# A softmax with relative-position bias: one row of one chunk loaded in 16 transfers of 15 to 1 partitions, first chunk in one transfer, bias table loaded once per 8 partitions

## The chip, the cores and the metric

One core of a Trainium2 chip runs the kernel. Its engines are VectorE (DVE in the profile), ScalarE (ACT), GpSimd (POOL), SyncE (SP) and TensorE (PE, not used here), and 16 DMA engines move data between HBM and the on-chip memory of 128 partitions. The metric is the device time in microseconds (us) of one execution; times of several runs are given as their median.

## What is computed

```python
B, H, S = (2, 8, 2112); max_rel = 16
rel = pos[:, None] - pos[None, :]
rel_clipped = np.clip(rel, -max_rel, max_rel) + max_rel
bias = rel_bias[:, rel_clipped]            # rel_bias: H x 33
logits = logits + bias[None]               # logits: B x H x S x S, float32
logits = logits - logits.max(axis=-1, keepdims=True)
exp = np.exp(logits)
return exp / exp.sum(axis=-1, keepdims=True)
```

It is a softmax over rows of 2112 elements, with a bias that depends on the head and on the distance between row and column, clipped at 16. Every element of the logits is read once and every element of the result is written once.

## The kernel before

The B x H x S = 33,792 rows are shared out evenly: each of the 128 partitions has ROWS = 264 consecutive rows of one head (PB = 8 partitions for each head and batch). A row is S = 2112 float32, 8448 bytes. The work goes in N = 44 chunks of R = 6 rows per partition; a chunk of all partitions is 6336 KB. Four buffers X[0] to X[3] (NBUF = 4) take the chunks in turn, and all is done in place.

**Order of the transfers.** All loads and stores are issued by SP, in program order. Before its loop SP issues the loads of the first four chunks. In the loop it issues the store of chunk n + 1 as soon as its rows are scaled (`store` takes the semaphore `scaled`), waits until the store of chunk n has landed (`st[b]`), and issues the load of chunk n + 4 into that buffer (`load`). The last chunk is stored in two halves.

**The first chunk** is loaded with six transfers of one row per partition (line 88). Five of them count on the semaphore `pre`, the sixth on `ld[0]`. VectorE takes `pre` before its loop (line 190), so it begins its loop when five rows are there. The other chunks come with one transfer each (line 78) that counts on `ld[b]`. Every transfer raises its semaphore by 16 in all when it has landed.

**The bias table.** ScalarE issues one transfer that copies the whole 8 x 33 table to each of the 128 partitions, into the tile F (line 97). GpSimd makes two small index tables. From these VectorE makes masks, keeps the head of each partition by a multiplication (line 131) and a sum over the heads (line 135, into rbS, 33 values), and builds the table M in the accumulation memory (lines 139 to 155): for each partition, the bias of every distance between row and column that occurs. `then` counts each instruction on the semaphore `dve` and `settle` waits for all so far.

**The loop.** VectorE, once for four chunks, copies a window of M to F (`strip`, line 160), so that each row's bias is a slice of F. Then for each chunk: `add` waits for `ld[b]` and runs one instruction per row that adds the bias and makes the row's negated maximum (line 166); ScalarE (`exps`, line 175) makes the exponential and its sum; `scale` on VectorE makes the reciprocals of three rows (line 183) and multiplies the rows by them (line 187).

Of the kernel before, what the change touches and what calls it, by code (L numbers as in the profile page):

```python
# [15 lines left out]
def kernel(  # L16
# [6 lines left out]
    nc = tc.nc  # L23
    P = 128
    B, H, S, S2 = logits.shape
    assert S == S2
    MR = 16
    W = 2 * MR + 1
    ROWS = B * H * S // P
    PB = S // ROWS  # L30
    assert ROWS * P == B * H * S and PB * ROWS == S and PB == H == 8
    R = 6
    NBUF = 4
# [4 lines left out]
    MW = S + ROWS - 1  # L38
    FW = S + STEP - 1
    BIG = 3.0e38  # L40

    io = ctx.enter_context(tc.tile_pool(name="io", bufs=1))
    X = [io.tile([P, R * S], FP32, tag=f"X{b}", name=f"X{b}") for b in range(NBUF)]
    F = io.tile([P, FW], FP32, tag="F", name="F")
    rbS = io.tile([P, W], FP32, tag="rbS", name="rbS")
# [3 lines left out]
    ip = io.tile([P, 3, PB], I32, tag="ip", name="ip")  # L49
# [3 lines left out]
    def view(t, offset, dims):  # L53

        return bass.AP(tensor=t.tensor, offset=t.offset + offset, ap=[[list(t.ap[0])[0], P]] + dims)

    def rows(t, j, n):

        return bass.AP(tensor=t.tensor, offset=t.offset + j * S, ap=[[ROWS * S, P], [1, n * S]])

    with tc.tile_critical(no_gpsimd_drain=True):
        ld = [nc.alloc_semaphore(f"ld{b}") for b in range(NBUF)]
# [3 lines left out]
        scaled = nc.alloc_semaphore("scaled")  # L66
        inv = nc.alloc_semaphore("inv")
        rb = nc.alloc_semaphore("rb")
        pre = nc.alloc_semaphore("pre")
        idx = nc.alloc_semaphore("idx")  # L70
        dve = nc.alloc_semaphore("dve")

        def take(eng, sem, n):
            eng.wait_ge(sem, n).then_inc(sem, -n)  # L74


        def load(j, b):
            nc.sync.dma_start(out=X[b][:, :], in_=rows(logits, j, R)).then_inc(ld[b], 16)
# [5 lines left out]
            ).then_inc(st[b], 16)  # L84


        for r in range(R):
            nc.sync.dma_start(
                out=X[0][:, r * S : (r + 1) * S], in_=rows(logits, r, 1)
            ).then_inc(ld[0] if r == R - 1 else pre, 16)  # L90
        for n in range(1, NBUF):
            load(n * R, n)

        rbB = view(F, 0, [[1, H * W]])
        nc.scalar.dma_start(
            out=rbB,
            in_=bass.AP(tensor=rel_bias.tensor, offset=rel_bias.offset, ap=[[0, P], [1, H * W]]),
        ).then_inc(rb, 16)  # L100
        nc.gpsimd.iota(ip[:, 0], pattern=[[0, PB]], base=0, channel_multiplier=1).then_inc(idx, 1)
        nc.gpsimd.iota(ip[:, 2], pattern=[[1, PB]], base=0, channel_multiplier=0).then_inc(idx, 1)  # L102

        v = nc.vector
        done = [0]

        def then(ins):
            done[0] += 1
            ins.then_inc(dve, 1)

        def settle():
            v.wait_ge(dve, done[0])

        SC = H * W
        mask = [F[:, SC + i * PB : SC + (i + 1) * PB] for i in range(9)]
        dp, dh, eq, hm, gt, le, lt, ra, rz = mask
        v.wait_ge(idx, 2)
        then(v.tensor_scalar(out=ip[:, 1], in0=ip[:, 0], scalar1=3, scalar2=7,  # L118
                             op0=ALU.logical_shift_right, op1=ALU.bitwise_and))
# [7 lines left out]
        for m, op in ((eq, ALU.is_equal), (gt, ALU.is_gt), (le, ALU.is_le), (lt, ALU.is_lt)):  # L127
# [4 lines left out]
            out=view(F, 0, [[W, H], [1, W]]), in0=view(F, 0, [[W, H], [1, W]]),  # L132
            in1=view(F, SC + 3 * PB, [[1, H], [0, W]]), op=ALU.mult))
        settle()
        then(v.tensor_reduce(out=rbS[:, :], in_=view(F, 0, [[1, W], [W, H]]),  # L135
                             axis=mybir.AxisListType.X, op=ALU.add))
        settle()
        low, high = rbS[:, W - 1 : W], rbS[:, 0:1]
        then(v.tensor_scalar(out=ra, in0=gt, scalar1=low, scalar2=None, op0=ALU.mult))  # L139
        then(v.tensor_scalar(out=rz, in0=gt, scalar1=low, scalar2=None, op0=ALU.mult))  # L140
        then(v.tensor_tensor(  # L141
            out=view(F, 0, [[W, PB], [1, W]]), in0=view(F, SC + 2 * PB, [[1, PB], [0, W]]),
            in1=view(rbS, W - 1, [[0, PB], [-1, W]]), op=ALU.mult))
# [6 lines left out]
            out=view(M, U, [[ROWS, PB], [1, W]]), in0=view(F, 0, [[W, PB], [1, W]]),  # L150
            in1=view(F, SC + 8 * PB, [[1, PB], [0, W]]), op=ALU.add))
        then(v.tensor_copy(out=view(M, U + W, [[ROWS, PB], [1, ROWS - W]]),  # L152
                           in_=view(F, SC + 7 * PB, [[1, PB], [0, ROWS - W]])))
        then(v.tensor_copy(out=M[:, 0:U], in_=low.to_broadcast([P, U])))  # L154
# [7 lines left out]
        def add(b):  # L162
            take(v, ld[b], 16)
            for r in range(b * R, (b + 1) * R):
                x = X[b][:, (r - b * R) * S : (r - b * R + 1) * S]
                v.tensor_tensor_reduce(  # L166
                    out=x, in0=x, in1=F[:, STEP - 1 - r : STEP - 1 - r + S], scale=-1.0, scalar=BIG,
                    op0=ALU.add, op1=ALU.min, accum_out=nmax[:, r : r + 1],
# [18 lines left out]
                    v.tensor_scalar_mul(out=x, in0=x, scalar1=rec[:, r : r + 1]).then_inc(scaled, 1)  # L187

        v.sem_inc(dve, -done[0])
        take(v, pre, 16 * (R - 1))  # L190
        with nc.Fori(0, ROWS - STEP + 1, STEP, engines=[ENG.DVE]) as j:  # L191
            strip(j)
            take(v, dve, 1)
# [51 lines left out]
```

## Time and profile before

| | |
|---|---|
| median of 3 runs | 1331.43 us (1330.2 to 1332.81) |
| span of the profiled execution, first to last instruction | 1327.7 us |
| VectorE busy | 976.6 us (74%) |
| ScalarE busy | 575.2 us (43%) |
| moved by the DMA engines | 571.11 MB, mean 430 GB/s over the span |
| HBM read, written | 285.61 MB, 285.47 MB |

The profile is of one execution. Its page gives the span of that execution and no device time of its own, so the span is the time that the lines add up to; the median of the runs is 3.7 us above it. In the page's slices each digit is the busy share of a fortieth of the span in tenths. The share of the DMA engines in a window is that of the packets that begin in it, so a short window can show over 1.00. A packet here is one contiguous piece that one DMA engine moves, or the 4 bytes with which it tells a semaphore that its part of a transfer is done.

### The profile page before, as it was taken

The page shows a single profiled execution, that of the slowest core. Times are in us where ns is not written, and L with a number is a line of the kernel's source. Part 1 is how long each engine was busy: PE and PEld are TensorE (multiplying, and loading weights), DVE is VectorE, ACT ScalarE, POOL GpSimd, SP SyncE. Part 2 cuts the span into 40 slices and gives each one's busy share as a digit, 9 for nine tenths or more (in the row PEclk, how much of TensorE's full clock was granted, in tenths as well). Part 3 has the DMA queues.
Part 4 walks back from the last instruction along what each step waited for, and adds up shares of the span by engine and source line. Part 5 has one row for each costly group of instructions (what it writes and reads, how often), then busy time and mean ns, then how long its engine had stood idle before and what let it go on. Part 6 is the DMA issues. An engine that isn't in the chain of part 4 may idle for free. (4 is left out here: it accounts for less than half of the span.)

```text
span 1327.7 us, 2454 instructions
## 1 busy us (share of the span) xinstructions
DVE 976.6 (74%) x911; ACT 575.2 (43%) x539; POOL 0.4 (0%) x6
## 2 busy tenths in 40 slices
DVE  6999667777777776687778777677877776687772
ACT  2564333444444343345444333444444343335440
POOL 0000000000000000000000000000000000000000
DMA  9999999999999999999999999999999999999998
GB/s 392 431 428 437 435 420 437 435 434 425 435 437 434 428 435 434 435 429 429 438 438 432 426 438 437 437 425 437 437 437 425 435 440 437 428 432 438 437 426 359
DMA packets 13683, 571.11 MB, mean 430 GB/s; under 512 B 1521, under 2 KB 1649, under 8 KB 1649
## 3 DMA queue, kind: packets, MB, share of 16 engines
q1 hardware_dynamic: 13536, 570.96, 99.6%
q10 hardware_dynamic: 144, 0.14, 0.1%
q14 instruction: 3, 0.02, 0.0%
HBM read 285.61 MB, written 285.47 MB: 430 GB/s over the span
## 5 line engine op out<-in xcount | busy, mean ns | idle before, releaser
L166 DVE CUSTOM_DVE_ANT_0 X<-X,F 128x2112 f32<-128x2112 f32 x264 | 605.2, 2354 | 301.3 <-DVEq L74 301.3
L175 ACT ACTIVATE X<-X,nmax 128x2112 f32<-128x2112 f32 x264 | 541.7, 2052 | 539.3 <-ACTq L74 517.6
L187 DVE TENSOR_SCALAR X<-X,rec 128x2112 f32<-128x2112 f32 x264 | 332.4, 1315 | 13.2
L175 ACT ACT_TABLE_LOAD x11 | 14.1, 1283 | 183.3 <-ACTq L74 183.3
L175 ACT ACTIVATION_READ_ACCUMULATOR X<-X,nmax 128x1 f32 x264 | 49.2, 186 | 0.0
L160 DVE COPY F<-M 128x2135 f32 x11 | 26.1, 2374 | 6.3 <-DVEq L74 6.3
L166 DVE DVE_READ_ACCUMULATOR2_ANT nmax<- 128x1 f32 x264 | 21.7, 82 | 0.0
L183 DVE RECIPROCAL rec<-tot 128x3 f32<-128x3 f32 x88 | 14.9, 170 | 0.0
L131 DVE TENSOR_TENSOR F<-F 128x264 f32<-128x264 f32 x1 | 0.4, 434 | 4.7 <-DMA F<-in_rel_bias_dram 4.7
L152 DVE COPY M<-F 128x1848 f32<-128x1848 f32 x1 | 2.1, 2077 | 0.0
L118 DVE TENSOR_SCALAR ip<-ip 128x8 int32<-128x8 int32 x1 | 0.2, 173 | 1.3 <-POOL ip L102 1.3
L135 DVE TENSOR_REDUCE rbS<-F 128x33 f32<-128x264 f32 x1 | 0.6, 610 | 0.0
L149 DVE TENSOR_TENSOR M<-F 128x264 f32<-128x264 f32 x1 | 0.4, 441 | 0.0
L141 DVE TENSOR_TENSOR F<-F,rbS 128x264 f32<-128x264 f32 x1 | 0.4, 425 | 0.0
L128 DVE TENSOR_SCALAR F<-F 128x8 f32<-128x8 f32 x4 | 0.4, 166 | 0.0
L154 DVE COPY M<-rbS 128x247 f32<-128x247 f32 x1 | 0.4, 408 | 0.0
L139 DVE TENSOR_SCALAR F<-F,rbS 128x8 f32<-128x8 f32 x1 | 0.2, 231 | 0.0
L145 DVE SCALAR_TENSOR_TENSOR F<-F,rbS 128x8 f32<-128x8 f32 x1 | 0.2, 225 | 0.0
L140 DVE TENSOR_SCALAR F<-F,rbS 128x8 f32<-128x8 f32 x1 | 0.2, 222 | 0.0
L146 DVE SCALAR_TENSOR_TENSOR F<-F,rbS 128x8 f32<-128x8 f32 x1 | 0.2, 219 | 0.0
L124 DVE TENSOR_TENSOR F<-ip 128x8 f32<-128x8 int32 x1 | 0.2, 167 | 0.0
L121 DVE TENSOR_TENSOR F<-ip 128x8 f32<-128x8 int32 x1 | 0.2, 166 | 0.0
(9 smaller groups left out, 1.2 us busy)
## 6 DMA issues: line engine op xcount, KB each, us to landing
X<-in_logits_dram SPq DMA_DIRECT2D x43, 6336.0 KB, 44.6
out_dram<-X SPq DMA_DIRECT2D x43, 6336.0 KB, 52.6
X<-in_logits_dram SPq DMA_DIRECT2D x6, 1056.0 KB, 12.1
out_dram<-X SPq DMA_DIRECT2D x2, 3168.0 KB, 21.1
F<-in_rel_bias_dram ACTq DMA_DIRECT2D x1, 132.0 KB, 6.2
```

What stands on the lines that cost most here:

```text
L128: then(v.tensor_scalar(out=m, in0=dp, scalar1=0.0, scalar2=None, op0=op))
L131: then(v.tensor_tensor(out=view(F, 0, [[W, H], [1, W]]), in0=view(F, 0, [[W, H], [1, W]]), in1=view(F, SC + 3 * PB, [[1, H], [0, W]]), op= ...
L135: then(v.tensor_reduce(out=rbS[:, :], in_=view(F, 0, [[1, W], [W, H]]), axis=mybir.AxisListType.X, op=ALU.add))
L141: then(v.tensor_tensor(out=view(F, 0, [[W, PB], [1, W]]), in0=view(F, SC + 2 * PB, [[1, PB], [0, W]]), in1=view(rbS, W - 1, [[0, PB], [-1, ...
L149: then(v.tensor_tensor(out=view(M, U, [[ROWS, PB], [1, W]]), in0=view(F, 0, [[W, PB], [1, W]]), in1=view(F, SC + 8 * PB, [[1, PB], [0, W]] ...
L152: then(v.tensor_copy(out=view(M, U + W, [[ROWS, PB], [1, ROWS - W]]), in_=view(F, SC + 7 * PB, [[1, PB], [0, ROWS - W]])))
L154: then(v.tensor_copy(out=M[:, 0:U], in_=low.to_broadcast([P, U])))
L160: v.tensor_copy(out=F[:, :], in_=M[:, bass.ds(ROWS - STEP - j, FW)]).then_inc(dve, 1)
L166: v.tensor_tensor_reduce(out=x, in0=x, in1=F[:, STEP - 1 - r : STEP - 1 - r + S], scale=-1.0, scalar=BIG, op0=ALU.add, op1=ALU.min, accum_ ...
L175: nc.scalar.activation(out=x, in_=x, func=EXP, scale=-1.0, bias=nmax[:, r : r + 1], accum_out=tot[:, r : r + 1],).then_inc(expd, 1)
L183: v.reciprocal(out=rec[:, r0 : r0 + HALF], in_=tot[:, r0 : r0 + HALF]).then_inc(inv, 1)
L187: v.tensor_scalar_mul(out=x, in0=x, scalar1=rec[:, r : r + 1]).then_inc(scaled, 1)
```

## The change

- The first chunk is loaded with one transfer, like the second and third. VectorE's wait for `pre` before its loop is gone.
- Chunk 3 is loaded in two parts. SP loads the first five of its six rows with one transfer, which now counts on `pre`. The sixth row comes in 16 transfers that ScalarE issues, of 15, 14, 13, 12, 11, 10, 9, 8, 8, 7, 6, 5, 4, 3, 2 and 1 partitions, in the order of the partitions (the list FAN). They count in turn on the semaphores `rest` and `fan`. GpSimd waits for both and for `pre`, and then raises `ld[3]`, on which VectorE waits for this chunk.
- The bias table is loaded to every eighth partition alone, 16 in place of 128. VectorE first clears the place in F with a memset, and ScalarE waits for that before it issues the transfer. After the sum over the heads, VectorE copies the result from each eighth partition to the other seven, with a transposition of 32 x 32 blocks, a copy that repeats each value 8 times, a second transposition and a copy into rbS.

The loop and the end are unchanged.

```diff
+    FAN = [15, 14, 13, 12, 11, 10, 9, 8, 8, 7, 6, 5, 4, 3, 2, 1]
+    assert sum(FAN) == P
...
-        for r in range(R):
-            nc.sync.dma_start(
-                out=X[0][:, r * S : (r + 1) * S], in_=rows(logits, r, 1)
-            ).then_inc(ld[0] if r == R - 1 else pre, 16)
-        for n in range(1, NBUF):
-            load(n * R, n)
-        rbB = view(F, 0, [[1, H * W]])
-        nc.scalar.dma_start(
-            out=rbB,
-            in_=bass.AP(tensor=rel_bias.tensor, offset=rel_bias.offset, ap=[[0, P], [1, H * W]]),
-        ).then_inc(rb, 16)
...
+        then(v.memset(F[:, 0 : H * W], 0.0))
+
+        nc.scalar.wait_ge(dve, 1)
+        nc.scalar.dma_start(
+            out=bass.AP(tensor=F.tensor, offset=F.offset, ap=[[PB * list(F.ap[0])[0], P // PB], [1, H * W]]),
+            in_=bass.AP(
+                tensor=rel_bias.tensor, offset=rel_bias.offset, ap=[[0, P // PB], [1, H * W]]
+            ),
+        ).then_inc(rb, 16)
+        LB = NBUF - 1
+        for n in range(LB):
+            load(n * R, n)
+        nc.sync.dma_start(
+            out=X[LB][:, 0 : (R - 1) * S], in_=rows(logits, LB * R, R - 1)
+        ).then_inc(pre, 16)
+        p = 0
+        for i, k in enumerate(FAN):
+            nc.scalar.dma_start(
+                out=X[LB][p : p + k, (R - 1) * S : R * S],
+                in_=bass.AP(
+                    tensor=logits.tensor, offset=logits.offset + (p * ROWS + LB * R + R - 1) * S,
+                    ap=[[ROWS * S, k], [1, S]],
+                ),
+            ).then_inc(fan if i % 2 else rest, 16)
+            p += k
...
+        take(nc.gpsimd, fan, 16 * (len(FAN) // 2))
+        take(nc.gpsimd, rest, 16 * (len(FAN) - len(FAN) // 2))
+        take(nc.gpsimd, pre, 16)
+        nc.gpsimd.sem_inc(ld[LB], 16)
...
+        Q = 32
+        RB, RT, RC, RW = [SC + 9 * PB + 2 * Q * i for i in range(4)]
+        then(v.memset(F[:, RB : RB + 2 * Q], 0.0))
...
-        then(v.tensor_reduce(out=rbS[:, :], in_=view(F, 0, [[1, W], [W, H]]),
+        then(v.tensor_reduce(out=F[:, RB : RB + W], in_=view(F, 0, [[1, W], [W, H]]),
                              axis=mybir.AxisListType.X, op=ALU.add))
+        settle()
+        then(v.transpose(out=F[:, RT : RT + 2 * Q], in_=F[:, RB : RB + 2 * Q]))
+        settle()
+        then(v.tensor_copy(out=view(F, RC, [[Q, 2], [PB, Q // PB], [1, PB]]),
+                           in_=view(F, RT, [[Q, 2], [PB, Q // PB], [0, PB]])))
+        settle()
+        then(v.transpose(out=F[:, RW : RW + 2 * Q], in_=F[:, RC : RC + 2 * Q]))
+        settle()
+        then(v.tensor_copy(out=rbS[:, :], in_=F[:, RW : RW + W]))
...
-        take(v, pre, 16 * (R - 1))
```

More of the change, by code (lines that the diff above doesn't have):

```diff
@@ L68 @@
         rb = nc.alloc_semaphore("rb")
-        pre = nc.alloc_semaphore("pre")
         idx = nc.alloc_semaphore("idx")
         dve = nc.alloc_semaphore("dve")
+        pre = nc.alloc_semaphore("pre")
+        fan = nc.alloc_semaphore("fan")
+        rest = nc.alloc_semaphore("rest")
         def take(eng, sem, n):
@@ L84, in store @@
             ).then_inc(st[b], 16)
-        for r in range(R):
-            nc.sync.dma_start(
-                out=X[0][:, r * S : (r + 1) * S], in_=rows(logits, r, 1)
-            ).then_inc(ld[0] if r == R - 1 else pre, 16)
-        for n in range(1, NBUF):
-            load(n * R, n)
-        rbB = view(F, 0, [[1, H * W]])
-        nc.scalar.dma_start(
-            out=rbB,
-            in_=bass.AP(tensor=rel_bias.tensor, offset=rel_bias.offset, ap=[[0, P], [1, H * W]]),
-        ).then_inc(rb, 16)
-        nc.gpsimd.iota(ip[:, 0], pattern=[[0, PB]], base=0, channel_multiplier=1).then_inc(idx, 1)
-        nc.gpsimd.iota(ip[:, 2], pattern=[[1, PB]], base=0, channel_multiplier=0).then_inc(idx, 1)
         v = nc.vector
@@ L112, in settle @@
             v.wait_ge(dve, done[0])
+        then(v.memset(F[:, 0 : H * W], 0.0))
[22 more added lines that the diff above has]
+            p += k
+        nc.gpsimd.iota(ip[:, 0], pattern=[[0, PB]], base=0, channel_multiplier=1).then_inc(idx, 1)
+        nc.gpsimd.iota(ip[:, 2], pattern=[[1, PB]], base=0, channel_multiplier=0).then_inc(idx, 1)
+        take(nc.gpsimd, fan, 16 * (len(FAN) // 2))
+        take(nc.gpsimd, rest, 16 * (len(FAN) - len(FAN) // 2))
+        take(nc.gpsimd, pre, 16)
+        nc.gpsimd.sem_inc(ld[LB], 16)
         SC = H * W
```

## The prediction

> **What bounds the kernel now.** I read the profile page first (span, busy times, the 40 slices, the DMA queues), then the busy time by window over the start and the end, then the DMA packets in short windows, and last the timeline of the first 45 us.
>
> ```profile
> span 1327.7 us, 2454 instructions
> DVE 976.6 (74%) x911; ACT 575.2 (43%) x539; POOL 0.4 (0%) x6
> DMA  9999999999999999999999999999999999999998
> q1 hardware_dynamic: 13536, 570.96, 99.6%
> q10 hardware_dynamic: 144, 0.14, 0.1%
> X<-in_logits_dram SPq DMA_DIRECT2D x43, 6336.0 KB, 44.6
> F<-in_rel_bias_dram ACTq DMA_DIRECT2D x1, 132.0 KB, 6.2
> ```
>
> No compute engine is full, while the 16 DMA engines are busy in all 40 slices, and the SP queue (q1) alone holds them for 99.6% of the span. All the traffic is needed: 571 MB. So a gain can come only from the stretches in which not all 16 run, and those are the two ends. The busy time by window (columns: window, length, DVE, ACT and POOL busy, clock, DMA share, GB/s), first the start and one long stretch of the middle, then the end:
>
> ```profile
> 0.00:2.00 2.00, 0.63 (x5) 0.00 (x0) 0.42 (x6) 1.00 0.00 2
> 2.00:4.00 2.00, 0.43 (x5) 0.00 (x0) 0.00 (x0) 1.00 0.87 168
> 4.00:6.00 2.00, 0.00 (x0) 0.00 (x0) 0.00 (x0) 1.00 0.87 280
> 6.00:8.00 2.00, 0.81 (x2) 0.00 (x0) 0.00 (x0) 1.00 0.96 396
> ...
> 60.00:1320.00 1260.00, 929.89 (x855) 548.67 (x514) 0.00 (x0) 1.00 1.00 433
> ```
>
> ```profile
> 1319.50:1320.50 1.00, 0.00 (x0) 0.00 (x0) 0.00 (x0) 1.00 1.00 431
> 1320.50:1321.50 1.00, 0.00 (x0) 0.00 (x0) 0.00 (x0) 1.00 0.42 177
> 1321.50:1322.50 1.00, 0.00 (x0) 0.00 (x0) 0.00 (x0) 1.00 0.53 228
> 1322.50:1323.50 1.00, 0.00 (x0) 0.00 (x0) 0.00 (x0) 1.00 0.41 177
> 1323.50:1324.50 1.00, 0.00 (x0) 0.00 (x0) 0.00 (x0) 1.00 0.35 152
> 1324.50:1325.50 1.00, 0.00 (x0) 0.00 (x0) 0.00 (x0) 1.00 0.12 51
> ```
>
> The middle is at 1.00 and 433 GB/s, which is 27.1 GB/s for each engine: a row of one partition (8448 B) is 0.31 us of one engine, a chunk of 6336 KB some 15.0 us of all. At the end the share falls in steps: the engines don't finish together. How they finish is seen in the packets under 512 B, since a transfer of this kernel ends with one such packet from each engine. Packets in the window 93.9 to 96.1 us, when the second store completes:
>
> ```profile
> DMA packets 33, 0.86 MB, mean 392 GB/s; under 512 B 16, under 2 KB 16, under 8 KB 16
> ```
>
> All sixteen within 2.2 us. At 587.5 to 588.5 and at 589 to 594 us (a load completes):
>
> ```profile
> DMA packets 23, 0.71 MB, mean 710 GB/s; under 512 B 9, under 2 KB 9, under 8 KB 9
> DMA packets 52, 2.28 MB, mean 456 GB/s; under 512 B 7, under 2 KB 7, under 8 KB 7
> ```
>
> And at the very end, 1320.5 to 1321.5, 1321.5 to 1323.5 and 1323.5 to 1326.5 us:
>
> ```profile
> DMA packets 16, 0.18 MB, mean 177 GB/s; under 512 B 9, under 2 KB 9, under 8 KB 9
> DMA packets 16, 0.41 MB, mean 203 GB/s; under 512 B 0, under 2 KB 0, under 8 KB 0
> DMA packets 15, 0.20 MB, mean 68 GB/s; under 512 B 7, under 2 KB 7, under 8 KB 7
> ```
>
> So nine engines keep step and are done at about 1321.0; seven fall behind in the first half of the run and finish 2.5 to 5.4 us later. I put the last at 1326.4, and the span ends 1.3 us after it. Equal shares of bytes, unequal ends: that tail is the one large thing to win. The shares from 1320.5 on add up to 1.83 us, and with half a packet in flight the sixteen would be done together at about 1322.8.
>
> **The change part by part.** *First chunk in one transfer, small bias load.* In the first 8 us the DMA engines move 2 x (2 + 168 + 280 + 396) = 1692 KB, which is 3.9 us at 433 GB/s; 4.1 us are lost. Two of these pass before any packet and stay. The other 2.1 us are the stretch in which 128 bias packets mix with one-row packets. The bias queue's 0.1% of the span is, unrounded, between 0.7 and 2.0 us of every engine; with 16 packets nearly all of it goes. Six one-row packets for one of six rows are a few hundredths each. But the fan's rows now mix with the first chunk. Bounds: nothing gained, and all 2.1; I take 1.0, nearer to the bias row's lower end.
>
> *The added bias work, the strip and the queues.* The timeline of the start:
>
> ```profile
> 0.92 0.41 ACTq L97 DMA_DIRECT2D F<-in_rel_bias_dram  x1
> 0.97 3.34 SPq L88 DMA_DIRECT2D X<-in_logits_dram  x6
> ...
> 7.16 0.43 DVE L131 TENSOR_TENSOR F<-F 128x264 f32<-128x264 f32 x1 [4.69 <-DMA F<-in_rel_bias_dram]
> ...
> 12.06 0.17 DVE L155 COPY M<-rbS 128x16 f32<-128x16 f32 x1
> 18.48 2.38 DVE L160 COPY F<-M 128x2135 f32 x1 [6.26 <-DVEq L74]
> 21.17 2.36 DVE L166 CUSTOM_DVE_ANT_0 X<-X,F 128x2112 f32<-128x2112 f32 x1 [0.31 <-DVEq L74]
> ...
> 23.65 1.28 ACT L175 ACT_TABLE_LOAD   x1 [23.65 <-ACTq L74]
> ...
> 43.07 22.23 SPq L82 DMA_DIRECT2D out_dram<-X  x2
> ```
>
> VectorE gets two memsets, two transposes and two copies. None has a row; the nearest are the 128x264 operation, 0.43 us, and the 128x16 copy, 0.17, so 1.0 to 2.6 us. ScalarE's bias load now waits for the first memset, about 1 us. Set-up ends by 16 us at worst, and the 6.26 us of idle before the strip copy cover it. That copy no longer waits for rows of chunk 0, so it is over before the chunk lands. Cost nothing; without that cover it would be the 1.0 to 3.6 us itself. ScalarE issues 17 transfers at 0.41 (its row) to 0.56 us each (3.34 / 6), until 8 to 11 us, and its first exponential is at 23.65: covered by 12 us. SP issues four loads in place of nine. GpSimd waits for the fan and for the five rows, then tells chunk 3's semaphore; only the end stands behind it in its queue, and at 22 us a chunk (21.17 to 43.07) VectorE comes to chunk 3 at 87 us, long after it has landed.
>
> *Chunk 0 later.* Its packets alternate on each engine with fan rows, at most one row per packet: 8 x 0.31 = 2.5 us on the lowest engines, less what the start gains. The first store slips from 43 to 45 us at most. The four loads keep the engines busy until 3 + 4 x 15 = 63 us. Cost nothing, with 18 us of cover.
>
> *The fan.* I read the 16 transfers as one row to each of k engines, always the lowest ones, since a transfer of this kernel is shared by its engines. Then the first engine gets 16 rows where an even split gives 8, the next 15, and so on to none on the last: from +2.5 to -2.5 us, in steps of 0.31. No row of this trace shows a transfer of fewer than 128 partitions, so this is an assumption, and one of the rivals is that it's wrong. [...]
>
> What the fan does to the end: the engines start apart by 5.0 us, about what the seven drift by themselves. As the drift has stopped by the second half, with nine engines in step and seven apart, I take it that engines in step push each other out of step, and that engines that are apart by this much are left alone. Then nobody drifts much; the fullest engine ends 2.5 us after the common front: 1321.0 + 2.5 - 1.0 (start) = 1322.5. I add 0.5 for some drift left and for the change between two queues, which gives 1323.0 where it was 1326.4: **-3.4 us**, span 1324.3. Bounds of this case: -1.5 (no gain at the start, 1 us more drift) to -4.6.
>
> **The rivals.**
>
> *B, crowding (slower).* Before, each engine carries its own partitions, all sixteen different. The fan gives 15 neighbouring partitions to 15 engines at the same moment. If four neighbours share a way into the on-chip memory that passes no more than the 27.1 GB/s of one engine, four rows take 4 x 0.31 us together, 0.94 more for each; 16 times on the first engine is 15 us. Engines part as they go, so I take half, 7.5: 1321.0 + 2.5 + 7.5 - 1.0 = 1330.0, against 1326.4, **+3.6 us** (up to +8). It decides from 0.25 us more per row: 16 x 0.25 = 4 us eats the gain. For it: the engines all run at the same 27.1 GB/s in loads and stores, as if a common width set it. Against: no row shows two engines at one neighbourhood, so nothing shows them hindering each other. [...]
>
> *C, no fan.* If a row goes to the engine that carries its partition anyway, every engine keeps its 8 rows and the nine-and-seven picture stays. Only the start is left: **-1.0 us**. For it: the split by partition is what the large transfers do, their engines being out of step for hundreds of us without hindrance. Against: little in the way they are issued.
>
> *D, drift on top.* If lateness itself makes an engine slip, the first engine starts 2.5 us late and falls 5.4 more: 1321.0 + 2.5 + 5.4 - 1.0 = 1327.9, **+1.5 us**, +2.5 or more if the start gives nothing. For it: the seven do fall behind ever further. Against: they stop, though they are then later than ever.
>
> **How the numbers follow.** The span is 1327.7 us and the median of the runs 1331.43, so 3.7 us lie around the span; the difference is put on the median. Likeliest is A: 1331.43 - 3.4 = 1328.0. Chances: A 0.48, B 0.37, C 0.08, D 0.07. The three runs of before lie within 0.2% (1330.2 to 1332.81), which is about what a measurement can tell; it is 2.7 us. Of A, 0.40 lies beyond that and 0.08 within. Of B, 0.30 is slower, 0.06 within, 0.01 faster. C gives 0.07 within and 0.01 faster, D 0.03 within and 0.04 slower. Together 0.42, 0.24 and 0.34. The range goes from -4.6 (1326.8) up into B, to +5.1 (1336.5); A by itself is 1326.8 to 1329.9.
>
> **What would show it.** A: the last sixteen small packets come in an even row over some 5 us, without the gap of 2 us, the last about 3 us earlier; one-row packets on ScalarE's queue last about 0.32 us; the share in the first 8 us is higher. B: the fan's transfers take far longer than their bytes, chunk 0 is begun after 24 us, the last engines end more than 8 us behind the first. C: nine and seven again. D: a tail longer than 6 us although the fan's rows are quick. If VectorE waits at the strip copy for the bias table, or the DMA share dips near 63 us, my covers were wrong. A span over 1327 us makes the forecast wrong.

## The result: slower, and where the time went

| | |
|---|---|
| before | 1331.43 us median (1330.2 to 1332.81, 5 runs) |
| after | 1338.96 us median (1338.26 to 1339.33, 5 runs) |
| ratio | 1.0054, 95% interval 1.0042 to 1.0066 |
| span of the profiled execution | 1327.7 before, 1337.2 after |

The change makes the kernel 7.5 us slower by the medians, and 0.54% slower by the ratio. The page of the changed kernel: span, busy share and rate of the DMA engines (two rows of 40 slices of 33.4 us), and the two queues.

```profile
span 1337.2 us, 2474 instructions
DMA  9999999999999999999999999999999999999997
GB/s 347 349 430 435 437 432 434 435 432 435 432 432 435 435 435 434 435 431 434 434 434 435 434 434 435 434 434 432 434 434 435 435 434 434 434 434 432 432 437 334
q1 hardware_dynamic: 12816, 569.87, 99.3%
q10 hardware_dynamic: 288, 1.10, 0.3%
```

The DMA engines are as busy as before in every slice, and yet in the first two slices they move only 347 and 349 GB/s. They don't wait for work; their packets take longer: those of 50,688 bytes that begin from 8 to 75 us last 2.29 us on average, where the kernel before has 1.88 (packet records). From 67 us on the rate is the full one, 430 to 437 GB/s up to the last slice. The busy time by window (columns as in the prediction), changed kernel:

```profile
2.00:4.00 2.00, 0.43 (x5) 0.00 (x0) 0.00 (x0) 1.00 1.29 406
4.00:6.00 2.00, 0.00 (x0) 0.00 (x0) 0.00 (x0) 1.00 0.94 406
6.00:8.00 2.00, 0.00 (x0) 0.00 (x0) 0.00 (x0) 1.00 0.96 414
...
8.00:62.00 54.00, 46.97 (x52) 26.51 (x25) 0.00 (x0) 1.00 1.02 353
62.00:75.00 13.00, 12.85 (x12) 6.08 (x5) 0.00 (x0) 1.00 0.98 398
```

and the kernel before in the two windows of the fan:

```profile
8.00:62.00 54.00, 46.73 (x49) 26.51 (x25) 0.00 (x0) 1.00 1.02 437
62.00:75.00 13.00, 13.00 (x12) 7.54 (x7) 0.00 (x0) 1.00 1.01 437
```

The start gains what it could: the first 8 us move 2 x (406 + 406 + 414) = 2452 KB where they moved 1692, which is 1.75 us at 433 GB/s. Then 54 x (1 - 353/437) + 13 x (1 - 398/437) = 10.4 + 1.2 = 11.6 us are lost: 9.8 more at the end of the first chunks, and the span grew by 9.5. (By the runs it is 7.5. The span of before lies 3.7 us below the median, that of after 1.8. Where a run has both on record, its time is 1.7 to 2.0 us above its span, so the profiled execution of before was some 1.8 us quicker than the median.) That accounts for the slowdown.

The drift is gone all the same. Small packets (one completion per engine and transfer) in windows of 2.2 us, first three when the first store completes (86.4 to 93.0 us), then four at the end (from 1327.9 us on):

```profile
DMA packets 27, 1.01 MB, mean 461 GB/s; under 512 B 7, under 2 KB 7, under 8 KB 7
DMA packets 24, 0.91 MB, mean 415 GB/s; under 512 B 6, under 2 KB 6, under 8 KB 6
DMA packets 21, 0.91 MB, mean 415 GB/s; under 512 B 3, under 2 KB 3, under 8 KB 3
...
DMA packets 32, 0.61 MB, mean 276 GB/s; under 512 B 8, under 2 KB 8, under 8 KB 8
DMA packets 13, 0.23 MB, mean 104 GB/s; under 512 B 4, under 2 KB 4, under 8 KB 4
DMA packets 6, 0.08 MB, mean 35 GB/s; under 512 B 3, under 2 KB 3, under 8 KB 3
DMA packets 2, 0.03 MB, mean 12 GB/s; under 512 B 1, under 2 KB 1, under 8 KB 1
```

The engines are some 6 us apart as soon as the first four chunks are in, without the hole that the nine-and-seven picture had. By the packet records of the trace (start, length and size of each packet) the sixteen lags, which are the times by which an engine ends a transfer after the first engine, are 0 to 6.2 us at 86 us and stay the same to some 2 ns for 1.2 ms, but for one engine that creeps on from 3.8 us and is the last. So engines that are apart do leave each other alone; but the first ends at 1327.5 us (just ahead of the four windows, which show the creeping engine twice) and the last at 1335.6, 8.1 us later, where it was 5.6 with the drift. Nothing is saved at the end.

The covers held. The timeline of the start, changed kernel:

```profile
2.01 6.42 ACTq L118 DMA_DIRECT2D X<-in_logits_dram  x16
...
15.12 0.17 DVE L187 COPY M<-rbS 128x16 f32<-128x16 f32 x1
15.77 2.38 DVE L192 COPY F<-M 128x2135 f32 x1 [0.48 <-DVEq L221]
22.77 2.36 DVE L198 CUSTOM_DVE_ANT_0 X<-X,F 128x2112 f32<-128x2112 f32 x1 [4.62 <-DVEq L78]
...
44.66 0.34 SPq L86 DMA_DIRECT2D out_dram<-X  x1
```

The bias table is ready at 15.3 us and VectorE then still waits 4.62 us for chunk 0; the first store goes at 44.7 us, far ahead of the end of the loads.

### The profile page after: what moved, and what is told of

It is laid out like the page before. It is cut to its first block, busy times and chain, and to the rows that moved or that the text cites. A ratio compares the mean times of both kernels' runs of the same rounds, so it can differ in the third digit from the quotient of the medians.

```text
span 1337.2 us, 2474 instructions
## 1 busy us (share of the span) xinstructions
DVE 977.8 (73%) x917; ACT 575.2 (43%) x539; POOL 0.4 (0%) x6
```

## The experiments

Every kernel was compared with the kernel before on the same chip, whose medians were 1330.13 us (for the first four kernels below), 1329.92 (the next four) and 1331.34 (the last three). The rate from 8 to 62 us, where the fan moves, is the measure of what a form of the sixth row costs. It is a rough one: a window counts the packets that begin in it, and one packet of 50,688 bytes more from each engine is 15 GB/s over 54 us. The packet records have a finer one, the lengths of the packets: 1.87 us for 50,688 bytes (six rows) and 0.32 us for one row where nothing hinders them. What the packets from 8 to 75 us last beyond that, per engine, is 11.4 us in the changed kernel and 0.2 in the kernel before; it is given below as "by packet lengths".

No trace names an engine or a partition. What follows takes it that the rows of a transfer go to the engines in order, one each, and calls an engine's *own place* what it writes in a transfer of rows 4 partitions apart that begins at one of the partitions 0 to 3 or 32 to 35. The runs show these transfers to be free: eight of them delayed no packet in the spread fan below, seven left the rate at 437 GB/s (seven extra), and eight went with 446 GB/s in eight and eight, where eight rows from 64 to 67 or from 96 to 99 on, by the same engines, cost about 0.5 us a transfer. That an engine's share of a transfer to 128 partitions goes to its own place too is an assumption, which the costs below fit. The expectations count four neighbours to a place; the 0.97 us that a transfer of 16 neighbours cost agrees with that.

**No fan.** Chunk 3 in one transfer, with GpSimd's waits for the fan gone too, the rest of the change kept:

```diff
-        nc.sync.dma_start(out=X[LB][:, 0 : (R - 1) * S], ...).then_inc(pre, 16)
-        for i, k in enumerate(FAN): ...
+        load(LB * R, LB)
```

> The changed kernel without the fan: chunk 3 in one transfer on SP's queue, the single first transfer and the small bias load kept. In the trace of the changed kernel the first 8 us move 2452 KB where they moved 1692 KB, which is 1.75 us of work, and the stretch from 8 to 75 us then loses some 9 us. Theory 1 (the fan's rows are what loses those 9 us): about 1331.4 - 1.75 = 1329.7 us, full rate from 3 us on, and at the end the nine-and-seven picture of before, with a drift of about 5.5 us. Rival (the single first transfer or the later bias load loses the time): 1337 us or more, with 350 GB/s in the first 60 us again.

Measured: 1331.79 us, ratio 1.0006 (0.9997 to 1.0016), span 1329.9. Windows 8 to 62 and 62 to 75 us, and the small packets at the end in 1319.8 to 1321.2, 1321.2 to 1324 and 1324 to 1329 us:

```profile
8.00:62.00 54.00, 50.77 (x56) 26.51 (x25) 0.00 (x0) 1.00 1.02 436
62.00:75.00 13.00, 13.00 (x12) 9.76 (x9) 0.00 (x0) 1.00 0.95 413
...
DMA packets 18, 0.18 MB, mean 127 GB/s; under 512 B 11, under 2 KB 11, under 8 KB 11
DMA packets 17, 0.41 MB, mean 145 GB/s; under 512 B 1, under 2 KB 1, under 8 KB 1
DMA packets 16, 0.28 MB, mean 56 GB/s; under 512 B 5, under 2 KB 5, under 8 KB 5
```

The fan is the loss: without it the rate is 436. But the start's 1.75 us did not come out at the end. At 62 to 75 us, when the first store follows the last of the first loads, 13 x (1 - 413/437) = 0.7 us go (0.9 by packet lengths), and the tail is longer than before: the last engine ends 8.6 us after the first (packet records), where it was 5.6. Ten engines, not nine, are in step at the end and six late.

**The sixth row in one transfer on ScalarE's queue.**

```diff
-        for i, k in enumerate(FAN): nc.scalar.dma_start(...)
+        nc.scalar.dma_start(
+            out=X[LB][:, (R - 1) * S : R * S], in_=rows(logits, LB * R + R - 1, 1)
+        ).then_inc(fan, 16)
```

> The sixth row of chunk 3 in one transfer of 128 partitions on ScalarE's queue, in place of the 16. It alternates with the first loads on every engine just as the fan does, 8 rows per engine, but every engine keeps its own partitions. Theory 1 (neighbouring partitions crowd at one place on the destination side): no loss, the time of the kernel without the fan within 0.5 us, the rows at about 0.32 us each, nine and seven at the end. Rival 2 (what costs is alternating between two queues, about 0.6 us per row on an engine): 8 x 0.6 = 5 us more than without the fan.

Measured: 1330.88 us, ratio 1.0002 (0.9992 to 1.0011).

```profile
8.00:62.00 54.00, 49.21 (x55) 26.51 (x25) 0.00 (x0) 1.00 1.02 435
```

Two queues that alternate on every engine cost nothing: each of the 128 rows lasts 0.32 us, but for the first few (0.37 at most). Rival 2 is out.

**The fan with partitions 4 apart**, the spread fan below. Same sizes in the same order, so the same rows per engine; PX is the step of one partition:

```diff
-    FAN = [15, 14, 13, 12, 11, 10, 9, 8, 8, 7, 6, 5, 4, 3, 2, 1]
+    FAN = [(15, 32), (14, 33), (13, 34), (12, 35), (11, 86), (10, 89), (9, 92), (8, 0), (8, 1), (7, 2), (6, 3), (5, 83), (4, 103), (3, 119), (2, 27), (1, 30)]
...
-                out=X[LB][p : p + k, (R - 1) * S : R * S],
+                out=bass.AP(tensor=X[LB].tensor, offset=X[LB].offset + q * PX + (R - 1) * S, ap=[[4 * PX, k], [1, S]]),
```

> The fan with the same sixteen sizes in the same order, and so the same rows per engine, but the partitions of one transfer are 4 apart and placed so that the long ones cross from partition 63 to 64: rows that move at the same time go to partitions far from each other. Theory 1 (crowding of neighbouring partitions): most of the 9 us go, chunk 3 is in at about 66 to 69 us on the last engine in place of 77.7, the drift stays away because the engines still start 5 us apart, and the time is 1327 to 1330 us, below both kernels. Rival 2 (alternating queues) and any rival in which the number of rows counts: 1338 us again.

Measured: 1330.9 us (1330.6 to 1331.33), ratio 1.0005 (0.9996 to 1.0015), span 1329.5.

```profile
8.00:62.00 54.00, 49.94 (x56) 26.51 (x25) 0.00 (x0) 1.00 1.01 411
62.00:75.00 13.00, 13.00 (x12) 8.94 (x9) 0.00 (x0) 1.00 1.03 439
```

Of 11.6 us lost, 54 x (1 - 411/437) = 3.2 are left (3.1 by packet lengths). In the packet records the first four transfers (15 to 12 rows) delay no packet at all, and neither do the four of 8, 8, 7 and 6 rows: in all eight each engine writes its own place. The three of 11, 10 and 9 rows lengthen one packet on all sixteen engines by about half a us, and four of the five smallest do so by 0.1 to 0.5 us: in these the engines write elsewhere. No two rows of one transfer are neighbours here, so a row away from its engine's own place costs time even without a neighbour in its transfer. The drift stays away. And yet the kernel is no faster than before: I had expected 1327 to 1330.

**Only the destination near.** The fan reads the rows of the spread layout, 4 partitions' stride apart, and writes neighbours as the changed kernel does; the sixth row of chunk 3 so holds other rows.

> The fan writes neighbouring partitions as in the changed kernel, but reads the rows that the spread layout reads, 4 partitions' stride apart in HBM, so the sixth row of chunk 3 holds other rows' logits and its results are not the reference's. Theory 1 (the crowding is on the destination side, in the on-chip memory): as slow as the changed kernel, 1337 to 1339 us. Rival 3 (it is the reads, sixteen rows 2.2 MB apart in HBM): as fast as the spread fan.

Measured: 1338.9 us, ratio 1.0064 (1.0048 to 1.0081).

```profile
8.00:62.00 54.00, 46.75 (x52) 26.51 (x25) 0.00 (x0) 1.00 1.01 353
```

The rate of the changed kernel to the digit. So where the rows are read from does not matter here, 353 GB/s either way; the cost is where they are written, as the 411 of the spread fan shows.

**Crowding without unequal shares.** Eight transfers of 16 partitions each, `q = 16 * i` with a step of 1, and then `q = i` with a step of 8:

```diff
+        for i in range(P // 16):
+            q = 16 * i   # second kernel: q = i, and 8 * PX, 8 * ROWS * S below
+            nc.scalar.dma_start(
+                out=bass.AP(tensor=X[LB].tensor, offset=X[LB].offset + q * PX + (R - 1) * S, ap=[[1 * PX, 16], [1, S]]),
+                in_=bass.AP(tensor=logits.tensor, offset=..., ap=[[1 * ROWS * S, 16], [1, S]]),
+            ).then_inc(fan, 16)
```

> The sixth row of chunk 3 in eight transfers of 16 neighbouring partitions: equal shares, one row per engine each, so no engine starts apart from the others, but four neighbours share a place. Theory 1 (four rows at one place go one after the other, and all 16 engines wait while they do): 0.94 us lost on every engine for each transfer, 8 x 0.94 = 7.5 us in the first 60 us, and the drift stays, since nothing sets the engines apart: 1331.8 + 7.5 = 1339 us. Rival (what costs in the fan is the unequal share, transfers on fewer than 16 engines): the time of the kernel without a fan, 1330 to 1332 us.

> [...] Theory 1: 0.31 us lost per transfer by that count, 2.5 us in all, or up to 0.55 each as the three crowded transfers of the spread fan showed, 4.4 us: 1334 to 1336 us. Rival (any two-way meeting is free): 1330 to 1332 us.

Measured: neighbours 1336.42 us, ratio 1.0045 (1.0028 to 1.0061); 8 apart 1332.37 us, ratio 1.0019 (1.001 to 1.0029). The two windows of the first, then of the second, then the small packets at the end of the first kernel in 1326.6 to 1327.4, 1327.4 to 1330.8 and 1330.8 to 1334.2 us:

```profile
8.00:62.00 54.00, 46.71 (x52) 26.51 (x25) 0.00 (x0) 1.00 1.01 372
62.00:75.00 13.00, 12.85 (x12) 5.81 (x5) 0.00 (x0) 1.00 1.03 446
...
8.00:62.00 54.00, 48.01 (x54) 26.51 (x25) 0.00 (x0) 1.00 1.00 398
62.00:75.00 13.00, 13.00 (x12) 7.13 (x7) 0.00 (x0) 1.00 1.06 460
...
DMA packets 13, 0.10 MB, mean 127 GB/s; under 512 B 9, under 2 KB 9, under 8 KB 9
DMA packets 25, 0.63 MB, mean 186 GB/s; under 512 B 0, under 2 KB 0, under 8 KB 0
DMA packets 17, 0.25 MB, mean 75 GB/s; under 512 B 7, under 2 KB 7, under 8 KB 7
```

With neighbours 54 x (1 - 372/437) - 13 x (446/437 - 1) = 7.8 us are lost by eight transfers, 0.97 each, where three times 0.31 us were expected; with rows 8 apart 4.8 - 0.7 = 4.1 us, 0.5 each, more than the 0.31 of the count and within the 0.55 of the expectation. (By packet lengths 8.1 and 4.4 us.) Equal shares don't save it, so unequal shares are not what costs; and in the first kernel, where nothing sets the engines apart, nine and seven are back. Both times are below what I had expected, 1336.42 against 1339 and 1332.37 against 1334 to 1336. By packet lengths neither kernel loses anything at the turn to stores, where the kernel without a fan lost 0.9 us, and the tail of the first is 7.3 us, not 8.6. The runs of the second reach from 1331.36 to 1335.41, and the profiled one, 1334.8, is among the slowest.

**Apart by extra rows.** Chunk 3 in one transfer, which SP issues after extra transfers of k rows each (every fourth partition, from 32, 33, 34 and 35 on in turn, so that each engine writes its own place), whose bytes it loads again:

```diff
+        EXTRA = [14, 12, 10, 8, 6, 4, 2]     # second kernel: 15 down to 1
+        for i, k in enumerate(EXTRA): nc.scalar.dma_start(...).then_inc(fan, 16)
+        take(nc.sync, fan, 16 * len(EXTRA))
+        load(LB * R, LB)
```

> Engines set apart without crowding: chunk 3 comes in one transfer again, but before it seven extra transfers of 14, 12, 10, 8, 6, 4 and 2 rows, 4 partitions apart from partition 32 on, load parts of that chunk that the whole transfer then loads again (SP waits for them before it issues it). The first engine moves 7 rows more than the last, 2.2 us. Theory 1: nothing lost by crowding, no drift if 2.2 us are apart enough, and the end at the front of the kernel without the fan plus 2.2 us: a span of 1323 to 1326 us, 1325 to 1328 us by the runs, below both kernels. Rival (2.2 us are not apart enough): drift as without a fan, 1331 to 1334 us.

> The same with fifteen extra transfers of 15 down to 1 rows: the engines are 4.7 us apart, as far as the fan sets them. Theory 1: no crowding, no drift, at the price of 15 more rows on the first engine: 2.5 us later than the extra-7 version if that has no drift, about 1328 to 1330 us. If the extra-7 version drifts and this one does not, the distance is what counts. Rival (drift comes whatever the distance): 1334 us or more.

Measured: seven extra 1329.78 us, ratio 0.9997 (0.9988 to 1.0007); fifteen extra 1337.3 us, ratio 1.0048 (1.0031 to 1.0065). With seven, from 8 to 62 and from 62 to 75 us, and then SP's queue with fifteen:

```profile
8.00:62.00 54.00, 50.05 (x56) 26.51 (x25) 0.00 (x0) 1.00 1.02 437
62.00:75.00 13.00, 13.00 (x12) 9.04 (x9) 0.00 (x0) 1.00 0.93 390
...
53.08 0.33 SPq L80 DMA_DIRECT2D X<-in_logits_dram  x1
53.53 0.35 SPq L84 DMA_DIRECT2D out_dram<-X  x1
```

With seven, the rate is whole while the rows move, and each row lasts 0.32 us, so these transfers on 14 to 2 engines, each at its own place, are free. But engines this far apart still drift: by the packet records the late ones go from 2.9 to 5.2 us, the creeping one to 6.1, and the end is where it was. The time lies between the two ranges that I had given. The second kernel missed its aim: the fifteen extra transfers take turns with the loads until 53 us, so that chunk 3 and the first store are issued too late (DMA share 0.66 from 50 to 60 us), the engines run dry, start together again and drift again. By the packet records they end the second chunk 4.3 us apart and the fourth 0.8. It tells nothing of the distance; it tells that this pause put the engines back in step.

**The two start changes apart.** Small bias load alone, and single first transfer alone, each in the kernel before:

> The kernel before with the small bias load alone: the first chunk in six transfers, no fan. It completes a square of four with the kernel before, the kernel without a fan (both start changes) and the next one. Theory (the single first transfer keeps the engines so well in step that all of them lose together when loads turn to stores, and drift further afterwards, as the kernel without a fan showed with 413 GB/s from 62 to 75 us where before had 437): this one keeps before's start and before's tail, -0.5 to -1 us for the bias packets, within 0.1% of the kernel before. Rival (the length of the drift has nothing to do with how the first chunk comes): its tail can be anything between 5 and 9 us.

> The kernel before with the single first transfer alone: the bias table still goes to 128 partitions, no fan. By the same theory: the start gains less than 1 us, the first turn from loads to stores loses 0.5 to 1 us, the tail is as long as without a fan (8.5 us): 0 to +2 us against before. Rival: the bias packets are what counts, and this one is as before.

Measured: small bias alone 1332.86 us, ratio 1.0014 (1.0005 to 1.0023); one first transfer alone 1331.64 us, ratio 1.0005 (0.9996 to 1.0014). From 62 to 75 us, first the small bias load, then the single transfer:

```profile
62.00:75.00 13.00, 13.00 (x12) 9.05 (x9) 0.00 (x0) 1.00 0.93 402
62.00:75.00 13.00, 12.85 (x13) 4.58 (x7) 0.00 (x0) 1.00 1.00 433
```

My theory falls: the kernel with rows first loses at the turn (1.0 us by packet lengths), the one with the single transfer doesn't. Their last engines end 10.0 and 8.0 us after the first, so neither part of the start change is worth anything by itself, and the smaller bias load even costs 0.14% here; on top of the single first transfer, in the kernel without a fan, it does not show. The loss at the turn goes with the bias load. By packet lengths every kernel with the small bias load and no rows at other engines' places loses 0.9 to 1.1 us there (no fan, the row in one transfer, seven and fifteen extra, small bias load alone), and the two with the table to 128 partitions lose nothing. Why stays open.

**Eight and eight.** 16 transfers of 8 rows, 4 partitions apart, all on the eight lowest engines; the first eight to the partitions 0 to 63, the others to 64 to 127:

```diff
+        for i in range(P // 8):
+            q = 32 * (i // 4) + i % 4
+            nc.scalar.dma_start(out=bass.AP(..., offset=X[LB].offset + q * PX + (R - 1) * S, ap=[[4 * PX, 8], [1, S]]), ...)
```

> The sixth row of chunk 3 in 16 transfers of 8 rows, 4 partitions apart, all on the eight lowest engines: 16 rows for each of these, none for the upper eight. The first eight transfers go to the places that the eight engines carry anyway, the next eight to the places of the other eight engines. Theory 1 with places of fixed width: the first eight cost nothing; of the next eight, each meets the upper engines' own packets, two at a place, and costs every engine 0.3 to 0.5 us, 2.5 to 4 us in all, so that the upper engines do not get ahead of the kernel without a fan though they have 8 rows less: 1332 to 1335 us, and the rate from 8 to 62 us is about 405 to 415 GB/s. Rival (an engine that has fewer rows is simply done earlier): no loss, the upper eight 2.5 us ahead, 1328 to 1330 us.

Measured: 1332.34 us, ratio 1.0008 (0.9999 to 1.0017). Three windows, the first while the transfers go to the lower engines' own places, the last while they go to the upper engines':

```profile
10.00:30.00 20.00, 17.75 (x24) 7.87 (x8) 0.00 (x0) 1.00 1.04 446
30.00:45.00 15.00, 14.70 (x15) 6.92 (x7) 0.00 (x0) 1.00 1.02 417
45.00:62.00 17.00, 16.70 (x18) 11.72 (x12) 0.00 (x0) 1.00 0.99 371
...
8.00:62.00 54.00, 49.95 (x56) 26.51 (x25) 0.00 (x0) 1.00 1.01 413
```

Own places cost nothing; the others cost 54 x (1 - 413/437) = 3.0 us by 62 us, to which six of the eight transfers contribute: 0.5 each, as much as in the kernel with 8 apart. (By packet lengths 3.3 us in all, from seven of them. The eighth, at 66 us, when the upper engines had their chunk 3, cost nothing.) All sixteen engines pay this. The first of the upper eight, with 8 rows less, ends chunk 3 at 63.0 us (packet records), 0.4 before the first engine of the kernel without a fan, whose last packet had just lost 0.5 at the turn to stores. So a net lead of 2.5 us is not there: the upper engines save 2.5 us of rows and lose 3.3 us while these rows go to their places.

The drift is gone here too, and yet the engines of each half start within 1.5 us of each other: but for the creeping one, the lags stay the same to some 10 ns from 93 us to the end. So eight engines in step do not push each other apart. In the kernels that drift, the drift leaves nine to eleven of them in step (within some 1.5 us).

## Why the prediction failed

**The step that failed** is the fan: "I take it that engines in step push each other out of step, and that engines that are apart by this much are left alone", with the end at 1321.0 + 2.5 - 1.0. Half of its mechanism held: the drift is gone in every kernel that has its engines 4 to 6 us apart from the start. That engines in step push each other apart is not shown, since eight and eight in step did not. What failed in the sum is a term that it put at nothing, the cost of getting the engines apart, and one engine that it did not know of.

*Getting apart was counted as free.* The likeliest case gave the fan's rows no cost at the destination, because no row showed one. That was the wrong way to choose between bounds so far apart (0 and 15 us). The rival with crowding had 0.94 us each time for four neighbours at one place; the runs give 0.97 per transfer of 16 neighbours. It was given too small a chance (0.37) and too small a price. I let the first engine alone pay, and half of the time. In fact every engine pays, also those that have no row in the transfer: in the packet records of the changed kernel, after the first transfer of 15 rows, the next packets of all sixteen engines last 2.35 to 3.07 us, 2.77 on average, in place of 1.87. Sixteen transfers lose 11.6 us, in place of 7.5 on one engine, and the net is +7.5 us by the runs and not +3.6. That four neighbours share a way was an assumption; the 0.97 us measured agree with it, as three more rows of 0.32 us take 0.96. The 0.31 us that I expected for each transfer of rows 8 apart is a count that no run shows; they cost 0.5 us. So did rows 4 apart that the engines wrote elsewhere (eight and eight), while at their own places they cost nothing (446 GB/s from 10 to 30 us there). Why engines that write elsewhere wait as well, no run shows.

*The lead of the emptiest engine* looks like a second failed term and is not one. The forecast has the engine without rows 2.5 us ahead of the common front, and no kernel shows that: the first engine of the spread fan ends at 1319.8 us, as that of the kernel without a fan does (1319.9). But the lead is only eaten by the crowding, which this engine pays like the others. With the measured terms the prediction's own sum (without the 0.5 us set aside for leftover drift) comes out: 1321.0 + 2.5 + 11.6 - 1.75 (start) = 1333.4 for the changed kernel, where the last engine but the creeping one ends at 1333.7; and 1321.0 + 2.5 + 3.2 - 1.75 = 1325.0 for the spread fan, where it ends at 1324.4.

*The engine that creeps* was in no term. It ends 1.9 us after all others in the changed kernel. In the spread fan it ends 3.5 us after them, at 1327.9, where the last engine of the kernel before ended at 1326.2. So the spread fan gains nothing because of this engine and of the 3.2 us of crowding that are left.

**The rest, point by point.** The start: 1.75 us in the first 8 us, within the bounds of 0 and 2.1; but the runs show that the kernel does not get faster by it. Covers: set-up by 16 us, measured 15.3; ScalarE's issues until 8 to 11 us, measured 8.4; first store by 45 us, measured 44.7. Rows to engines: one row to each of the lowest k; the packet records of the changed kernel show 15 engines with a row in the first transfer, 14 in the second and so on (that they are the lowest, no trace shows), and the rival without a fan is out. Of the signs I named for crowding, slow rows (up to 0.89 us) came; so did a spread of 8 us at the end, but by luck, as the creeping engine makes it (6.2 without it). Chunk 0 was begun at 22.77 us, before the 24 that I gave, as only the first two or three transfers crowd in the first 20 us. Drift on top of lateness did not come, but for the one engine.

## What to carry to other kernels

When the DMA engines are the bound, read their rate next to their share: a share of 1.0 at 353 in place of 437 GB/s meant here packets that hindered each other (2.29 us in place of 1.88), not missing work. Transfers over few partitions cost nothing here (up to eight in a row) where each engine wrote its own place, as defined above (437 GB/s); partitions side by side in a transfer of one row per engine made all engines wait 0.97 us each time. Before shifting work between engines, ask whether what limits them is the engine or the place that the bytes go to.

## What the hardware showed that I had not expected

- The sixteen DMA engines drift apart while loads and stores take turns, by 5.6 to 10.0 us in 1.3 ms, most of it in the last packet of a load (86% of the lengthening from 115 to 465 us in the kernel before, 62% without a fan); engines that are apart by 4 to 6 us from the start, or in two halves 5 us apart, keep their distance to some 50 ns, but for one. With the drift gone the runs also differ less: 1330.6 to 1331.33 us for the spread fan against 1328.66 to 1331.99 for the kernel before on the same chip. (The kernel with seven extra transfers, which drifts, differs as little, 1329.33 to 1330.3.)
- One engine of the sixteen loses about 50 ns per transfer in every trace with the engines apart: 3.8 to 8.0 us behind the first in 81 transfers of the changed kernel. In eight and eight it ends 4.0 us after all others. Whether it does so outside a profiled execution was not tried.
